# Where a layer's large tiles start in SBUF, and when its v, bias tables and combination take their turn

## The chip, the cores and the metric

One core of one Trainium2 chip. The metric is the time of one execution on the device in microseconds; smaller is better. The kernel before has a median of 1522.92 us over 3 runs (1522.58 to 1523.85).

## The reference

One layer of an encoder on 1024 tokens of width 1024, all in fp32. Cut to what matters:

```python
mod = silu(c) @ w_ada + b_ada                        # six vectors: sh1, sc1, gt1, sh2, sc2, gt2
h = rms_norm(x, g_norm1) * (1 + sc1) + sh1
qa, ka, va, qb, kb, vb, gates = split(h @ w_in)
o_a = neighbourhood_attention(rms(qa), rms(ka), va, rpb)      # 8 heads, bias, column mask
outs, lses = three dilated windows of rotary(rms(qb)), rotary(rms(kb)), vb    # 4 heads each
o_b = sum over windows of softmax(lses) * outs               # the combination
ga, gb = split(sigmoid(gates + b_gate))
x = x + gt1 * ((ga * (o_a @ w_proj_a) + gb * (o_b @ w_proj_b)) @ w_o)
h2 = rms_norm(x, g_norm2) * (1 + sc2) + sh2
a, up = split(h2 @ w_ffn_in)
x = x + gt2 * ((silu(a) * up) @ w_ffn_out)
```

## The kernel before, in words

Every large product is made of fp32r matmuls (a faster fp32 form) in three passes: each operand is split into a rounded part and the rest, whi and wlo for weights (`wsplit`, L108 on ACT and L109 on DVE or POOL), hT[0] and hT[1] for activations, and PASS multiplies high by high, high by low and low by high. In `nc.tensor.matmul(out, a, b)` the tile a is loaded into TensorE (PE) and b streams through it, 384 or 512 columns of 4 bytes.

The stages, in order of time:

- A prologue (to about 60 us) reads x and the first conditioning weights, and makes hT.
- Units 0 to 9, steps n = 6 to 79 of one loop (`u, t = divmod(n, 8)`, L897): in each step `proj_chunk` (L293) makes q, k and v of one token tile for the current unit, eight chunks of three matmuls with 384 columns of whi or wlo streaming. Between the chunks stands the attention of the unit before: `at_scores` (L451, L518: qk streams), `at_qk` (softmax, L465 to L469), the transposes of P (L477), `at_pv` (L492). At the end of a step `proj_post` normalizes q and k and stores v to v_d (L333); at t == 7 it loads the whole unit's v back (L344, eight DMAs for most units). Units 0 to 5 are the dilated windows (kinds 0 to 2), 6 to 9 the neighbourhood attention (kind 3), whose scores get a bias table rb per head (L398, 128x768). From step 58 on (PAIRED) each step has scores; a unit's scores begin two steps after its projections end.
- Beside this, `ada_step` runs once a step: it loads two rows of the conditioning weights (tile wa2, L276, 512 KB; the profile calls it wa) and multiplies them into acc2 on DVE (L280, L282; acc in the profile).
- The combination of the three windows: `combine_prep` loads a piece of the outputs (L626 to L633) and spreads its weights (fb), `combine_step` transposes fb on PE (four transposes, L647, into bank t) and multiplies. Twelve pieces, one a step, from `n - 63`: prep in steps 63 to 74, step in 64 to 75.
- Gates: L687, L706 (hT or tg stream); merge: L1095 (oT streams); output projection: L1237 (whi, wlo or wr streams); feed-forward: L1301 (h2T or t streams, whi or wlo is loaded) and L1471 (whi and wlo stream).

PE, ACT, DVE, POOL and SP (the DMA queue) take their instructions in an order fixed when the program is built; for the loop above a list scheduler sets that of ACT, DVE, POOL and SP, with priorities by the order of the code and `urgent`. A DMA into a tile waits on SP until the tile is free, and holds what is queued behind it. Eight buffers of 4096 bytes a partition, tag "big", hold v, rb, wa2, the pieces tp, gsig and oacc in turn; a tile that is asked for later takes its buffer later.

Where the tiles lie in SBUF (byte offset in each partition, modulo 512, in the built programs):

| tiles | before | addresses before | after |
|---|---|---|---|
| hT, h2T, raw, whi, wlo, x, x2 | 320 | 2,368 to 121,152 | 0 |
| qk, v, wa2, rb, PT, acc2, tp | 352 | 123,232 to 227,680 | 0 |
| P, stg | 416 | 191,392 to 205,728 | 0 |
| tg, sg, oT, wr, t, e, c, m | 480 | 139,232 and up | 0 |
| xt, tm, gt1, qn, rtab | 0 | 146,944 and up | 0 |
| ident | 448 | 1,472 | 448 |

Of the kernel before, what the change touches and what calls it, by code (L numbers as in the profile page):

```python
# [10 lines left out]
F32 = mybir.dt.float32  # L11
# [20 lines left out]
LATE, NPRE = (3, 4, 5, 6, 7), 12  # L32
KFIRST, KLAST, OT = (3, 4, 2, 0, 5, 6, 1, 7), (2, 0, 1, 3, 4, 5, 6, 7), 3
PP, QT, AQ, AT, AV = 100, 0, 0, 0, 0
WARM = 40
PAIRED = 58
XSQ = "avavaaaa"
XSC = "ddddvvvv"
XE = ("av", "vv", "aa", "aa", "vv", "aa", "va", "va")
# [3 lines left out]
def hybrid_layer(ctx: ExitStack, tc: tile.TileContext, x, colp, wada1, wada2, bada2, wqkv, wg, wpa, wpb,  # L43
                 wo, w1, w2, hgain, ropeg, rope, rbias, bmask, g2r, out):
    nc = tc.nc

    def pool(name, side, **kw):
        return tc.alloc_tile_pool(name=name, bufs=1, side=side, reuse_waits="tile", **kw)

    const = pool("const", "left")  # L50
    wp = pool("w", "left")
    ctx.enter_context(tc.manual_schedule(engines={mybir.EngineType.PE}))
    ps = tc.alloc_tile_pool(name="ps", bufs=2, space=bass.MemoryType.PSUM)
# [10 lines left out]
    x2_d = tc.dram_tile([S, D], F32, name="x2_d")  # L64
    w1_d = tc.dram_tile([2, 4, 128, 512], F32, name="w1_d")
    e_d = tc.dram_tile([6, 2, 128, 512], F32, name="e_d")

    def bank(tag):
        return ps.tile([128, 512], F32, tag=tag, name="ps_" + tag)
# [22 lines left out]
    nc.vector.tensor_mul(cact, cact, c_c)  # L92
    bg1 = const.tile([128, 8], F32, name="bg1")
    nc.vector.scalar_tensor_tensor(bg1, bsc1, 1.0, g1_c, op0=ALU.add, op1=ALU.mult)

    def fview(ap):
        return ap.bitcast(F32)
# [17 lines left out]
    def rstd(p, n, width, ss, tag):  # L115
        v = p.tile([128, width], F32, tag="rv", bufs=3, name="rv")
        y = p.tile([128, width], F32, tag="ry", bufs=3, name="ry")
        z = p.tile([128, width], F32, tag="rz", bufs=3, name="rz")
        nc.scalar.activation(y, ss, AF.Ln, scale=1.0 / n, bias=eps)  # L119
        nc.vector.tensor_scalar(v, ss, 1.0 / n, EPS, op0=ALU.mult, op1=ALU.add)  # L120
        nc.scalar.activation(y, y, AF.Exp, scale=-0.5)
        nc.vector.tensor_mul(z, y, v)
        nc.vector.scalar_tensor_tensor(z, z, -0.5, y, op0=ALU.mult, op1=ALU.mult)
        nc.vector.scalar_tensor_tensor(y, z, 1.5, y, op0=ALU.add, op1=ALU.mult)
        return y
# [7 lines left out]
    ap_ = pool("attn", "right")  # L133
# [7 lines left out]
    def big(name, shape=None, dtype=F32):  # L141
        return ap_.tile(shape or wide, dtype, tag="big", bufs=NBIG, name=name)

    yT = [ap_.tile([128, 4, S], F32, tag="qk", bufs=2, name="yT") for _ in range(2)]
    land = [big("land") for _ in range(NLAND)]
    seq = [0]

    def landing():
# [30 lines left out]
    pw = bank("t")  # L179
    for i in range(WARM):  # L180
        nc.tensor.transpose(pw[:, :128], ident, ident)
# [55 lines left out]
    rtab = []  # L237
# [8 lines left out]
                                        rg[:, qk, f, None, :].to_broadcast([128, 8, 16]), op=ALU.mult)  # L246
        return tb

    rg = const.tile([128, 2, 2, 16], F32, name="rg")
    nc.sync.dma_start(rg, ropeg)  # L250
    bm = ap_.tile([128, 512], F32, tag="bm", bufs=1, name="bmask")
    nc.sync.dma_start(bm, bmask)
# [43 lines left out]
    def urgent(off):  # L296
        def deco(f):
            def g(*a):
                with tc.high_priority(off):
                    return f(*a)  # L300
            return g
        return deco

    @urgent(PP)
    def proj_post(U, t):
        pd = U.pd[t]
        qn = ap_.tile([128, 4, 64], F32, tag="qn", bufs=7, name="qn")
        U.qn[t] = qn
        pq = pd[:, :256].rearrange("p (h d) -> p h d", h=4)
        sq = ap_.tile([128, 256], F32, tag="sq", bufs=1, name="sq")  # L310
        nc.scalar.activation(sq, pd[:, :256], AF.Square)
        nc.scalar.activation(qn, pq, AF.Copy)
        ss = ap_.tile([128, 4], F32, tag="ss4", bufs=2, name="ss4")
        nc.vector.tensor_reduce(ss, sq.rearrange("p (h d) -> p h d", h=4), axis=mybir.AxisListType.X, op=ALU.add)  # L314
        r = rstd(ap_, 64, 4, ss, "q")
        nc.vector.tensor_tensor(qn, qn, r[:, :, None].to_broadcast([128, 4, 64]), op=ALU.mult)  # L316
        if U.kind < 3:
            ra = ap_.tile([128, 4, 16], F32, tag="ra", bufs=2, name="ra")
            rb = ap_.tile([128, 4, 16], F32, tag="rb", bufs=2, name="rb")
            tb = U.tab[:, t]  # L320
            v4 = lambda z: z.rearrange("p (a b) c -> p a b c", a=2)
            tv = lambda f, c0, c1: tb[:, f, :, None, c0:c1].to_broadcast([128, 2, 2, c1 - c0])
            nc.gpsimd.tensor_tensor(v4(ra), v4(qn[:, :, 0:16]), tv(0, 0, 16), op=ALU.mult)  # L323
            nc.gpsimd.tensor_tensor(v4(rb[:, :, 0:8]), v4(qn[:, :, 8:16]), tv(1, 0, 8), op=ALU.mult)
            nc.gpsimd.tensor_tensor(v4(rb[:, :, 8:16]), v4(qn[:, :, 0:8]), tv(1, 8, 16), op=ALU.mult)
            nc.gpsimd.tensor_tensor(qn[:, :, 0:16], ra, rb, op=ALU.add)
        if U.kind == 0:
            nc.scalar.activation(U.v[:, t, :], pd[:, 256:384], AF.Copy)
        else:
            vs = ap_.tile([128, 128], F32, tag="vs", bufs=2, name="vs")  # L330
            nc.scalar.activation(vs, pd[:, 256:384], AF.Copy)  # L331
            vd = v_d[U.u - 2]
            nc.sync.dma_start(vd[t * 128:(t + 1) * 128, :], vs)  # L333
            if t == 7 and U.kind == 1:
                vv = vd.rearrange("(h i r) d -> h i r d", h=2, r=4)
                uv = U.v.rearrange("p (r h) d -> p h r d", h=2)
                for j in range(2):
                    nc.sync.dma_start(uv[:, j], vv[j])
            elif t == 7 and U.kind == 2:
                nc.sync.dma_start(U.v, vd.rearrange("(i u) d -> i u d", u=8))  # L340
            elif t == 7:
                vv = vd.rearrange("(r j c) d -> j c r d", r=16, c=8)
                for j in range(8):
                    nc.sync.dma_start(U.v[:, j, :], vv[j])  # L344
# [37 lines left out]
    def new_unit(u, w):  # L382
        U = Unit()
        U.kind, U.pair = UNITS[u]
        U.u = u
        U.w = w
        U.pd, U.qn = {}, {}
        qk = ap_.tile([128, 4, S], F32R, tag="qk", bufs=2, name="qk")
        U.qk = [qk[:, i, :] for i in range(4)]
        U.v = big("v", [128, 8, 128])  # L390
        if U.kind < 3:
            U.tab = rtab[0] if rtab else None
            U.st = ap_.tile([128, 9, 4], F32, tag="st", bufs=2, name="st")
        else:
            U.bias = []
            for h in range(2):
                b = big("rb", [128, 768])
                nc.sync.dma_start(b, rbias[U.pair * 2 + h])  # L398
                U.bias.append(b)
        return U  # L400

    class Item:
        pass
# [347 lines left out]
    extra = {}  # L751
    w0 = []
    U = new_unit(0, w0)
    units.append(U)
    rowk = {}
# [134 lines left out]
    for t in range(6):  # L890
        proj_post(U, t)
# [5 lines left out]
    for n in range(6, 92):  # L897
        u, t = divmod(n, 8)
        if u < 10:
            if t == 0:  # L900
                units.append(new_unit(u, [nextw[u, k] for k in range(KT)]))
            U = units[u]
            chunks = [lambda k=k, U=U, t=t: proj_chunk(U, t, k) for k in range(KT)]
        elif n - 80 < NPRE:
            chunks = gate_pre(n - 80)
        else:
            chunks = []
# [11 lines left out]
                    ready.setdefault(8 * u + 2 + slot, []).append(I)  # L919
        if n == 8 * 7 + 5:  # L920
            combine_stats()
        ci = n - (8 * 7 + 7)
        if 0 <= ci < 12:
            combine_prep(ci)
        if n >= PAIRED:
            done, prev, cur = prev, cur, ready.pop(n, [])
# [9 lines left out]
        def chunk():  # L936
            if chunks:
                chunks.pop(0)()
                k = 8 - len(chunks)
                if t == 7 and u + 1 < 10 and k < 8 and k >= 2:  # L940
                    nextw[u + 1, k] = wsplit(raws[u + 1, k], nc.vector if k % 2 else None)

        turns = [(units[0], tt) for tt in {8: (0, 1), 9: (2, 3), 11: (4, 5), 13: (6, 7)}.get(n, ())]
        if PAIRED <= n <= 81 or 9 < n < PAIRED and n % 2:
            turns += [(units[m // 8], m % 8) for m in ((n - 2,) if n >= PAIRED else (n - 3, n - 2)) if m >= 8]
        chunk()
# [3 lines left out]
        if n < 10:  # L950
            while chunks:
                chunk()
        if n >= PAIRED or n % 2 or n < 10:
            for I in cur:
# [35 lines left out]
            chunk()  # L990
        if u < 10:
            proj_post(U, t)

    def gate_first(i, eng):
        for q, nm in enumerate(("w11", "w12")):
            gwt[i, nm] = wsplit(gate_raw(i, q), eng)
# [188 lines left out]
    wop = pool("wo", "right")  # L1185
# [45 lines left out]
    for t in range(8):  # L1231
# [8 lines left out]
                o_turn(t - 2)  # L1240
        o_post(t, pbs)

    wj = {}

    gt = {}
# [285 lines left out]
    fp.release()  # L1531
    ps.release()
    wp.release()
    const.release()


# [98 lines left out]
```

## Time and profile before

| what | us |
|---|---|
| median of the runs | 1522.92 |
| the profiled execution's own time | 1524.07 |
| its span | 1522.3 |
| PE busy | 1499.0 |
| DVE busy | 1101.9 |
| ACT busy | 657.4 |
| POOL busy | 538.4 |

The mean granted clock of PE was 0.998. Matmuls are pipelined: the duration of one contains part of the one before, so their price is read from start to start. Bracketed times in the timeline are the wait ahead of an instruction, with what ended it. By stretches the span divides into the prologue (0 to 60), units with dilated attention (60 to 350), units with neighbourhood attention and the combination (350 to 520), gates (520 to 710), merge and output projection (710 to 875), and the feed-forward product (875 to 1522).

### The profile page before, as it was taken

Reading aid. Unit: us, or ns where it says so; the run is one execution under the profiler, and the core shown is the slowest. Engines: PE = TensorE matmul, PEld = TensorE weight load, DVE = VectorE, ACT = ScalarE, POOL = GpSimd, SP = SyncE. Lnnn points to the kernel's source line nnn. Section 1 sums busy time; section 2 is a strip of 40 time slices with the busy share of each in tenths; the row PEclk is TensorE's granted clock in tenths of the full one; section 3 lists DMA queues with packets and bytes.
Section 4 is the critical chain, followed back from the end, with each engine's and each line's share of the span. In section 5 each row is a group of like instructions: output and inputs, shape, how many; then the busy total and the mean of one; then the engine's idle time right before and its main releaser. Section 6 shows DMA issues by size and latency. Waiting matters only on the chain. (4 is left out here: it accounts for less than half of the span.)

```text
span 1522.3 us, 24290 instructions
## 1 busy us (share of the span) xinstructions
PE 1499.0 (98%) x8156; PEld 1267.7 (83%) x8156; DVE 1101.9 (72%) x2318; ACT 657.4 (43%) x1638; POOL 538.4 (35%) x540
## 2 busy tenths in 40 slices
PE   9999999999999999999999999999999999999998
PEld 7999989998888877788888888888888888887886
DVE  6868777767899845466665596788777777599468
ACT  5555555554544543236432354333222233344442
POOL 0432333311101040002342301677777775104464
PEclk9999999999999999999999999999999999999999
DMA  9625544535245165824562225345533334798342
GB/s 369 231 76 184 158 148 150 175 124 166 73 138 149 61 202 155 304 83 126 165 217 101 93 89 177 127 132 170 174 107 104 105 107 141 268 365 285 99 153 97
DMA packets 154414, 241.66 MB, mean 159 GB/s; under 512 B 26656, under 2 KB 73376, under 8 KB 153520
## 3 DMA queue, kind: packets, MB, share of 16 engines
q1 hardware_dynamic: 153136, 235.90, 47.5%
q10 hardware_dynamic: 1152, 4.19, 0.7%
q8 instruction: 65, 1.06, 0.3%
q14 instruction: 61, 0.50, 0.1%
HBM read 179.89 MB, written 60.15 MB: 158 GB/s over the span
## 5 line engine op out<-in xcount | busy, mean ns | idle before, releaser
L109 POOL TENSOR_TENSOR wlo<-raw,whi 128x512 fp32r<-128x512 f32 (+2 forms) x133 | 173.0, 1314 | 469.4 <-ACT whi L108 417.6
L108 ACT ACTIVATE whi<-raw 128x512 fp32r<-128x512 f32 (+1 forms) x348 | 204.3, 600 | 282.7 <-PE ps_s L1471 33.6
L293 PE MATMUL ps_d<-whi,hT 128*128 128x384 f32 x1152 | 311.7, 342 | 0.3 <-ACT vs L331 0.3
L109 DVE TENSOR_TENSOR wlo<-raw,whi 128x512 fp32r<-128x512 f32 (+1 forms) x215 | 181.8, 857 | 77.2 <-ACT whi L108 72.0
L293 PEld LDWEIGHTS ps_d<-whi,hT 128*128 128x128 f32 x1152 | 210.4, 189 | 5.8 <-ACT vs L331 4.1
L293 PE MATMUL ps_d<-wlo,hT 128*128 128x384 f32 x576 | 193.9, 337 | 2.2 <-DVE wlo L109 1.9
L293 PEld LDWEIGHTS ps_d<-wlo,hT 128*128 128x128 f32 x576 | 109.0, 189 | 3.0 <-DVE wlo L109 2.2
L108 ACT ACTIVATE whi<-ws 128x512 fp32r<-128x512 f32 x65 | 40.9, 629 | 130.3 <-DVE ws L1318 76.6
L1251 POOL TENSOR_TENSOR e<-e,c 128x512 f32<-128x512 f32 x44 | 68.6, 1560 | 64.3 <-DVE c L1381 40.1
L109 POOL TENSOR_TENSOR wlo<-m,whi 128x512 fp32r<-128x512 f32 x35 | 51.6, 1484 | 54.0 <-ACT whi L108 54.0
L323 POOL TENSOR_TENSOR ra<-qn,rtab 128x64 f32<-128x64 f32 x48 | 16.2, 338 | 150.8 <-DVE qn L316 132.1
L530 ACT ACTIVATE P<-P,st 128x256 f32<-128x256 f32 (+2 forms) x100 | 45.5, 456 | 40.6 <-DVE st L528 40.6
L687 PE MATMUL ps_d<-hT,whi 128*128 128x512 f32 x192 | 60.5, 396 | 0.0
L1301 PE MATMUL ps_v<-h2T,whi 128*128 128x512 f32 x192 | 59.3, 390 | 0.0
L1301 PE MATMUL ps_s<-h2T,whi 128*128 128x512 f32 x192 | 59.2, 390 | 0.0
L466 ACT ACTIVATE P<-P,sx 128x384 f32<-128x384 f32 (+1 forms) x64 | 37.0, 578 | 51.4 <-DVE sx L465 51.4
L1249 ACT ACTIVATE e<-e 128x512 f32<-128x512 f32 x44 | 27.4, 630 | 71.9 <-DVE e L1384 47.4
L282 DVE SCALAR_TENSOR_TENSOR acc<-wa,cact,acc 128x512 f32<-128x512 f32 x56 | 42.0, 749 | 20.6 <-DMA wa<-in_wada_dram 20.4
L1301 PE MATMUL ps_d<-h2T,whi 128*128 128x512 f32 x184 | 56.8, 390 | 0.0
L109 DVE TENSOR_TENSOR wlo<-ws,whi 128x512 fp32r<-128x512 f32 x45 | 50.5, 1123 | 8.2 <-ACT whi L108 8.2
L119 ACT ACTIVATE ry<-ss,eps 128x4 f32<-128x4 f32 (+1 forms) x88 | 26.3, 299 | 67.4 <-DVE ss L314 65.2
L1250 DVE TENSOR_TENSOR e<-e 128x512 f32<-128x512 f32 x44 | 42.6, 975 | 17.3 <-ACT e L1249 17.1
(445 smaller groups left out, 3968.9 us busy)
## 6 DMA issues: line engine op xcount, KB each, us to landing
raw<-in_w_dram SPq DMA_DIRECT2D x139, 256.0 KB
ga_d<-e SPq DMA_DIRECT2D x77, 256.0 KB
raw<-ga_d SPq DMA_DIRECT2D x77, 256.0 KB
wa<-in_wada_dram SPq DMA_DIRECT2D x32, 512.0 KB
raw<-in_wqkv_dram SPq DMA_DIRECT2D x80, 192.0 KB
m<-in_w_dram SPq DMA_DIRECT2D x44, 256.0 KB
raw<-in_wg_dram SPq DMA_DIRECT2D x42, 256.0 KB
xt<-in_x_dram SPq DMA_DIRECT2D x16, 512.0 KB
```

Source lines behind the costliest of these rows:

```text
L108: nc.scalar.activation(hi[:, :n], r, AF.Copy)
L109: (eng or nc.gpsimd).tensor_sub(lo[:, :n], r, fview(hi[:, :n]))
L119: nc.scalar.activation(y, ss, AF.Ln, scale=1.0 / n, bias=eps)
L282: nc.vector.scalar_tensor_tensor(ada_acc[c], wa, cact[:, kk:kk + 1], ada_acc[c], op0=ALU.mult, op1=ALU.add)
L293: nc.tensor.matmul(pd[:, :384], tok(a, k, t), U.w[k][b][:, :384], start=(k == 0 and i == 0), stop=(k == KT - 1 and i == 2))
L466: nc.scalar.activation(P[:nq, :nk], P[:nq, :nk], AF.Exp, scale=-1.0, bias=nm, accum_out=sm)
L530: nc.scalar.activation(C.P[h][:nq, c], C.P[h][:nq, c], AF.Exp, scale=-1.0, bias=nm, accum_out=sm)
L687: nc.tensor.matmul(st["p"], gw[i, br][j][a][:, kk * 128:(kk + 1) * 128], hT[b][:, k, hs], start=(k == 0 and q == 0), stop=(k == 7 and q == 2))
L1249: nc.scalar.activation(sg, a, AF.Sigmoid)
L1250: nc.vector.tensor_mul(sg, sg, a)
L1251: nc.gpsimd.tensor_mul(sg, sg, up)
L1301: nc.tensor.matmul(pb, w[p][:, k * 128:(k + 1) * 128], b[q][:, k], start=(k == 0 and i == 0), stop=(k == 3 and i == 2))
```

## The change

Four edits, cut to their core:

```diff
+EDGE, CFILL, AFILL, OFILL = 480, 192, 384, 32
-PAIRED = 58
+PAIRED, RBT, COMB = 58, 5, 64
...
+    edge = pool("edge", "right")
+    edge.tile([128, EDGE // 4], F32, name="edge")
...
+    def fill(p, n, name):
+        p.tile([128, n // 4], F32, name=name)
...
+    rg = const.tile([128, 2, 2, 16], F32, name="rg")
+    fill(const, CFILL, "cfill")
...
+    for tag, n, bufs in (("bm", 512, 1), ("p", 512, 4), ("qn", 256, 7), ("rtab", 512, 1), ("acc2", 512, 1), ("pT", 512, 4),
+                         ("stg", 512, 3), ("vs", 128, 2), ("ra", 64, 2), ("rb", 64, 2)):
+        ap_.tile([128, n], F32, tag=tag, bufs=bufs, name="place")
...
+            if t == 7:
+                U.v = big("v", [128, 8, 128])
             if t == 7 and U.kind == 1:
...
-        U.v = big("v", [128, 8, 128])
+        if U.kind == 0:
+            U.v = big("v", [128, 8, 128])
...
             U.bias = []
-            for h in range(2):
-                b = big("rb", [128, 768])
-                nc.sync.dma_start(b, rbias[U.pair * 2 + h])
-                U.bias.append(b)
...
+    def bias_tabs(U):
+        for h in range(2):
+            b = big("rb", [128, 768])
+            nc.sync.dma_start(b, rbias[U.pair * 2 + h])
+            U.bias.append(b)
...
-        ci = n - (8 * 7 + 7)
+        ci = n - COMB
...
             proj_post(U, t)
+            if U.kind == 3 and t == RBT:
+                bias_tabs(U)
+
+    fill(ap_, AFILL, "afill")
...
+    fill(wop, OFILL, "ofill")
```

1. Unused tiles (edge, cfill, afill, ofill) and the list of tags taken early, large before small, put every large tile at a multiple of 512 bytes. Nothing writes or reads them.
2. v takes its big buffer just ahead of its load at t == 7 instead of at the unit's start (kind 0, which writes it from PSUM, excepted).
3. The two bias tables of a kind-3 unit are allocated and loaded at the end of its step 5 instead of at its start.
4. The combination's pieces stand one step later: prep in steps 64 to 75, step in 65 to 76.

The order on POOL is the same as before. On PE only the transposes of the combination move. Lines of the new program are 10 to 18 higher (L276 becomes L288, L282 L294, L293 L305, L465 L482, L398 L416, L344 L358, L647 L664).

On SP, around the turn from unit 6 to unit 7 (v and v_d are the unit's values, rb the bias tables, wa2 the conditioning weights, u_d a window's output), before:

```order
L344 DMA v_4679<-v_d_72 128x1x128 x8
L333 DMA v_d_72<-vs_5360 128x128
L398 DMA rb_5310<-in_rbias_dram 128x768
L398 DMA rb_5312<-in_rbias_dram 128x768
L276 DMA wa2_5341<-in_wada2_dram 128x1024
L573 DMA u_d_70<-stg_5387 128x512
L333 DMA v_d_72<-vs_5429 128x128
L276 DMA wa2_5486<-in_wada2_dram 128x1024
L276 DMA wa2_5666<-in_wada2_dram 128x1024
```

and after:

```order
L358 DMA v_5314<-v_d_76 128x1x128 x8
L345 DMA v_d_76<-vs_5370 128x128
L288 DMA wa2_5351<-in_wada2_dram 128x1024
L590 DMA u_d_74<-stg_5397 128x512
L288 DMA wa2_5496<-in_wada2_dram 128x1024
L288 DMA wa2_5676<-in_wada2_dram 128x1024
L345 DMA v_d_76<-vs_5439 128x128
L416 DMA rb_5815<-in_rbias_dram 128x768
L416 DMA rb_5817<-in_rbias_dram 128x768
L288 DMA wa2_5910<-in_wada2_dram 128x1024
```

Here the three wa2 loads moved ahead of the two rb loads, the first of them to the place of the first rb.

On DVE in step 59, where the first of these wa2 tiles is used (acc2 is the running sum; rz, ry and qn belong to the normalization of q and k; the ISA rows read the scores of two heads with their bias; P is the softmax), before:

```order
L123 SCALAR_TENSOR_TENSOR rz_5421<-rz_5421,ry_5420 128x4
L124 SCALAR_TENSOR_TENSOR ry_5420<-rz_5421,ry_5420 128x4
L316 TENSOR_TENSOR qn_5413<-qn_5413,ry_5420 128x256
L465 ISA P_5455,sx_5456<-ps_s_5447,rb_4680 128x256
L465 ISA sx_5456 128x1
L465 ISA P_5461,sx_5462<-ps_s_5448,rb_4682 128x256
L465 ISA sx_5462 128x1
L379 SCALAR_TENSOR_TENSOR qk_5308<-ps_v_5467,hg_83,qk_5308 128x2x64
L380 TENSOR_TENSOR qk_5308<-ps_v_5467,qk_5308 128x2x64
L468 RECIPROCAL sx_5456<-sx_5456 128x1
L282 SCALAR_TENSOR_TENSOR acc2_5119<-wa2_5341,cact_96,acc2_5119 128x512
L469 TENSOR_SCALAR P_5455<-P_5455,sx_5456 128x256
```

and after:

```order
L133 SCALAR_TENSOR_TENSOR rz_5431<-rz_5431,ry_5430 128x4
L294 SCALAR_TENSOR_TENSOR acc2_5129<-wa2_5351,cact_100,acc2_5129 128x512
L134 SCALAR_TENSOR_TENSOR ry_5430<-rz_5431,ry_5430 128x4
L482 ISA P_5465,sx_5466<-ps_s_5457,rb_5150 128x256
L482 ISA sx_5466 128x1
L482 ISA P_5471,sx_5472<-ps_s_5458,rb_5152 128x256
L482 ISA sx_5472 128x1
L294 SCALAR_TENSOR_TENSOR acc2_5129<-wa2_5351,cact_100,acc2_5129 128x512
L328 TENSOR_TENSOR qn_5423<-qn_5423,ry_5430 128x256
L393 SCALAR_TENSOR_TENSOR qk_5323<-ps_v_5477,hg_87,qk_5323 128x2x64
L394 TENSOR_TENSOR qk_5323<-ps_v_5477,qk_5323 128x2x64
L485 RECIPROCAL sx_5466<-sx_5466 128x1
```

The first use of the tile moved from behind both score passes to ahead of ry.

On PE in step 64 (whi and wlo stream against hT; fb holds the combination's weights), before:

```order
L293 MATMUL ps_d<-whi,hT_106 128x384
L293 MATMUL ps_d<-wlo,hT_106 128x384
L293 MATMUL ps_d<-whi,hT_391 128x384
L647 MATMUL ps_t<-ident,fb 128x128 x4
L293 MATMUL ps_d<-whi,hT_106 128x384
```

and after, the same place:

```order
L305 MATMUL ps_d<-whi,hT_112 128x384
L305 MATMUL ps_d<-wlo,hT_112 128x384
L305 MATMUL ps_d<-whi,hT_406 128x384
L305 MATMUL ps_d<-whi,hT_112 128x384
L305 MATMUL ps_d<-wlo,hT_112 128x384
```

The four transposes are gone from this step; the row x4 stands in each of the steps 65 to 76 now.

More of the change, by code (lines that the diff above doesn't have):

```diff
@@ L247, in rope_tab @@
         return tb
-    rg = const.tile([128, 2, 2, 16], F32, name="rg")
     nc.sync.dma_start(rg, ropeg)
@@ L1533, in hybrid_layer @@
     wp.release()
+    edge.release()
     const.release()
```

## The prediction

> **What bounds the kernel now.** I read the page's busy times first, then the stretches, then the matmul groups with shapes kept apart, then the timeline of single matmuls, and last the list of waits. The page says that TensorE (PE) is nearly the whole span, at an almost full clock:
>
> ```profile
> span 1522.3 us, 24290 instructions
> PE 1499.0 (98%) x8156; PEld 1267.7 (83%) x8156; DVE 1101.9 (72%) x2318; ACT 657.4 (43%) x1638; POOL 538.4 (35%) x540
> PEclk9999999999999999999999999999999999999999
> ```
>
> By stretches (the columns are busy time and instructions of PE, its weight loads, DVE, ACT and POOL, then granted clock, DMA share, GB/s):
>
> ```profile
> 350.00:520.00 170.00, 162.40 (x1140) 143.35 (x1139) 147.34 (x490) 87.59 (x293) 14.41 (x13) 0.99 0.41 124
> 700.00:760.00 60.00, 60.00 (x260) 48.48 (x259) 42.84 (x59) 31.93 (x48) 24.84 (x20) 1.00 0.49 156
> 760.00:860.00 100.00, 100.00 (x454) 81.63 (x453) 57.40 (x100) 29.58 (x68) 32.96 (x20) 1.00 0.39 139
> 950.00:1360.00 410.00, 410.00 (x1783) 334.94 (x1782) 309.25 (x363) 131.81 (x223) 252.44 (x175) 1.00 0.48 158
> ```
>
> The reader is to see two kinds of time. From 700 on PE is busy without a gap while DVE has 101 of 410 us to spare, POOL 158 and DMA half: there only the length of a matmul counts, and a shorter one shortens the kernel at once. From 350 to 520 (units 6 to 9, with the combination) PE waits 7.6 us and DVE is busy 87%: there the order of other engines counts. The change touches both, so I cost them apart. A difference of 0.2%, 3.0 us, is about what a measurement of this kernel can tell from no change.
>
> **Edit 1: large tiles at multiples of 512 bytes.** It adds no instruction but unused memory. What it can alter is how long an instruction reads or writes a tile. In the matmul groups the operand behind "<-" that comes first is the one that streams through (512 columns of the tile), the second is the loaded one; the last number is the mean ns.
>
> ```profile
> L293 PE MATMUL ps_d<-whi,hT 128*128 128x384 f32 x1152 | 311.7, 342 | 0.3 <-ACT vs L331 0.3
> L1301 PE MATMUL ps_v<-h2T,whi 128*128 128x512 f32 x192 | 59.3, 390 | 0.0
> L1301 PE MATMUL ps_d<-t,whi 128*128 128x512 f32 x136 | 42.8, 396 | 0.0
> ...
> L1301 PE MATMUL ps_s<-t,whi 128*128 128x512 f32 x128 | 40.3, 396 | 0.0
> ...
> L1301 PE MATMUL ps_v<-t,wlo 128*128 128x512 f32 x68 | 27.0, 397 | 0.0
> ...
> L1301 PE MATMUL ps_t<-t,wlo 128*128 128x512 f32 x64 | 25.4, 396 | 0.0
> ...
> L1237 PE MATMUL ps_d<-wr,h2T 128*128 128x512 f32 x90 | 22.4, 398 | 0.0
> ...
> L1095 PE MATMUL ps_v<-oT,whi 128*128 128x512 f32 x64 | 20.2, 397 | 0.0
> ...
> L706 PE MATMUL ps_v<-hT,whi 128*128 128x512 f32 x48 | 14.8, 389 | 0.0
> ...
> L706 PE MATMUL ps_d<-tg,whi 128*128 128x512 f32 x40 | 12.6, 396 | 0.0
> ```
>
> One line, L706, issues the same matmul from hT in 389 ns and from tg in 396; L1301 does so from h2T and t. By their places in memory (front part), hT, h2T, whi and wlo start at 320 past a multiple of 512, tg, t, oT and wr at 480. 320 is a multiple of 64, 480 is not. These durations overlap, since matmuls are pipelined, so the price is read from starts:
>
> ```profile
> 949.33 0.62 PE L1301 MATMUL ps_d<-h2T,whi 128*128 128x512 f32 x2
> ...
> 951.37 0.63 PE L1301 MATMUL ps_s<-t,whi 128*128 128x512 f32 x2
> ...
> 956.91 0.63 PE L1301 MATMUL ps_v<-t,whi 128*128 128x512 f32 x2
> ...
> 959.72 0.63 PE L1301 MATMUL ps_d<-t,whi 128*128 128x512 f32 x2
> ```
>
> From 949.33 to 951.37 stand nine matmuls from h2T: 2.04 / 9 = 226.7 ns from start to start. From 956.91 to 959.72 stand twelve from t: 2.81 / 12 = 234.2 ns. The tile at 480 costs some 7 ns more each. How many there are: from t 136 + 136 + 128 + 128 on whi and half as many on wlo (each pass runs twice on whi, once on wlo), 792; from wr 90 + 90 + 60 = 240; from oT 288 and from tg 180, of which the rows above are the largest groups. Together 1,500, and 1,500 x 7 ns = 10.5 us. The difference in a start is known to about 1 ns, so 9 to 12. All lie in stretches where PE has no gap, or next to it, so I count all of it; DVE's and POOL's slack above covers a step that is 3% shorter.
>
> The score matmuls read qk, now at 352, also not a multiple of 64:
>
> ```profile
> L451 PE MATMUL ps_s<-qk 64*128 64x384 f32 x144 | 19.0, 368 | 0.0
> ```
>
> With L518's and the smaller groups they are 492 matmuls of 64 rows, which run in pairs, 246 pairs. The start of what they read varies inside the tile, and no row has the same form at another place. From nothing to the full 7 ns a pair is 0 to 1.7 us; I take the middle, 0.9.
>
> The rest, the tiles at 320 that go to 0, I cost at nothing, because 320 is already a multiple of 64 and the matmuls from it are the shorter. That is a choice; the first rival is its failure. DVE, ACT and POOL read and write the same tiles; their groups of 128x512 at 320 and at 480 differ by no step that I could see, and PE would hide it from 700 on.
>
> **Edits 2 to 4: the order in units 6 to 9.** v's big buffer is taken later, but its load stays where it was on SP's queue. What moves is what else waits on those buffers. The bias tables rb (two of 393 KB) go from the start of a unit to its sixth step, behind the wa loads instead of ahead. Step 59 shows what that order costs now (the bracket is the wait ahead of the instruction):
>
> ```profile
> 364.87 0.90 SPq L398 DMA_DIRECT2D rb<-in_rbias_dram  x2
> 365.87 0.37 SPq L276 DMA_DIRECT2D wa<-in_wada_dram  x1
> ```
> ```profile
> 371.93 0.75 DVE L282 SCALAR_TENSOR_TENSOR acc<-wa,cact,acc 128x512 f32<-128x512 f32 x1 [4.39 <-DMA wa<-in_wada_dram]
> ```
> ```profile
> 373.01 0.44 PE L477 MATMUL ps_t<-ident,P 128*128 128x128 f32 x2 [1.77 <-DVE P L469]
> 374.32 0.44 PE L477 MATMUL ps_t<-ident,P 128*128 128x128 f32 x2 [0.88 <-DVE P L469]
> ```
>
> SP, done with v's eight pieces, issues rb and then wa. wa arrives 6 us after its issue, acc waits 4.39 us for it on DVE, and P, behind acc, holds PE's transposes for 1.77 + 0.88 = 2.65 us. Now wa is issued where rb was, 1.0 us earlier (365.87 - 364.87), with 786 KB less ahead of it. That speaks for a gain of up to these 2.65 us, plus what the clock lost after it, which I estimate at 1 to 2 us. But the new order on DVE puts acc earlier too (front part): ry, qn and both score passes, which it stood behind, now stand behind acc. If wa lands 2 us earlier and acc stands 2 us earlier, the wait is as long as before and only falls on other work. Gain 3, loss 3 at the ends; I take 1.0, since the issue is earlier for sure. The rb loads come five steps before the first scores that read them (a unit's scores begin two steps after its end): hidden.
>
> The combination begins at step 65 instead of 64. Step 64 also carries the last weight splits of the next unit and the load of v:
>
> ```profile
> 414.90 0.66 PE L647 MATMUL ps_t<-ident,fb 128*128 128x128 f32 x4 [1.67 <-ACT PT L483]
> ```
>
> The first four transposes of L647 wait 1.67 us for a bank that ACT frees. Moved on, they meet a step with less in it: 1.5 us gained, if nothing else is late in step 64. In exchange the last combination lies in step 76, which now has one piece more; 0 to 1 us lost if that step waits too, which DVE's 87% allows. Its output is read only by L1095's oT after 700. Together the order edits are worth 2.5 us, between a gain of 6.5 (both waits and their clock) and a loss of 4.
>
> **Sum.** The profiled execution took 1524.07 us (span 1522.3), 1.15 above the median of the runs, 1522.92. 1524.07 - 10.5 - 0.9 - 2.5 = 1510.2; against the median, 1509.0. By the ends of the terms: 1522.92 - 12 - 1.7 - 6.5 = 1502.7 and 1522.92 - 9 + 4 = 1517.9.
>
> **Rivals.** *First, the granule is coarser than 64 bytes, and the tiles at 320 pay as well.* Then the 226.7 ns would also fall. A second step of 7 ns for the L293 matmuls (1,152 from whi, 576 from wlo), the 1,056 from h2T, those of L1471 (924) and the other tiles at 320 (some 800), 4,500 in all, is 31.5 us, and 7 more on the 1,500 is 10.5: 1509 - 42 = 1467. No large tile that streams through PE starts at 0 now, so the trace has no row against it; for it speaks only that 226.7 ns has no reason of its own here. I hold it less likely, because the one step that the rows show is used up between 320 and 480. The Trainium skill, TensorE: Matmul & The Clock Gate, section "Wait — 56ns, not 53.3ns?", gives 215.7 ns from start to start for 512 columns when warm (measured there on bf16); this trace has 226.7 at its best place, so by that page 11 ns would still be open on every matmul, about 66 us over 6,000, as an estimate. Nothing here shows whether the type or the place makes that gap. From 1475 down the producers would begin to bind (DVE is at 309 of 410 us), so I give this case 1445 to 1480. Chance 0.17.
>
> *Second, the address modulo 64 isn't the reason.* The tiles with the longer matmuls all lie in the upper half of the memory (t from 139,232 up), the others below 122,000; the trace cannot tell which property does it. If it is the half, edit 1 is worth nothing, and with -2.5 to +1 of the order the time is 1520.4 to 1524; I say 1521.5. By the Trainium skill, SBUF — State Buffer, section "Specifications (TRN2)", SBUF is read in lines of 16 bytes: 320 and 480 are both multiples of 16, so by that rule the two would cost the same and edit 1 would bring nothing; the rows above, 389 against 396 ns on one line, show that something beyond that rule separates them. Chance 0.13.
>
> *Third, slower: acc becomes a wait ahead of everything.* wa competes with v's eight pieces and lands as late as now. DVE reaches acc before ry, qn, scores and P, and the whole 4.39 us goes to PE with some 1.5 us of lost clock, 5.9 us, in each of the three units 7, 8 and 9: 17.7. Against the 11.4 of edit 1 that is +6.3: 1529. It decides when wa lands more than 4 us after DVE gets to acc in all three. The wait row above speaks for it; that wa is issued ahead of rb speaks against. Chance 0.08.
>
> **How the numbers follow.** The forecast has 0.62, own range 1503 to 1518; the rivals 0.17, 0.13 and 0.08. Faster by over 0.2%: 0.62 + 0.17 and a little of the second, 0.80. Within: nearly all of the second, 0.12. Slower: the third, 0.08. The range leaves out the first rival (0.17) and the far end of the third, and takes in the others: 1502 to 1527.
>
> **What would show it.** Right: the groups of t, tg, oT and wr at 389 to 390 ns, the twelve matmuls of 956.91 at 2.72 us; L293 unchanged at its pitch; the stretch from 700 to 1360 shorter by about 9 us, that from 350 to 520 by 2 to 3, with no wait of L647 in step 64. Wrong: L1301 from h2T or L1471 shorter than now (first rival), t still at 396 (second), acc waiting longer on wa and PE's wait in 350 to 520 above 7.6 us (third).

## The result, and the profile after

Five runs of the changed kernel took 1509.84 us in the median (1508.57 to 1516.15), against 1522.92 (1522.58 to 1524.86) for five of the kernel before: a ratio of 0.9921, with an interval of 0.9900 to 0.9942. The profiled execution took 1508.57 us. The page of the changed kernel:

```profile
span 1506.8 us, 24296 instructions
PE 1486.2 (99%) x8156; PEld 1265.3 (84%) x8156; DVE 1098.1 (73%) x2318; ACT 656.3 (44%) x1638; POOL 537.1 (36%) x540
```

The span is 15.5 us shorter; PE is busy 12.8 us less with the same 8,156 matmuls. The matmul groups with shapes kept apart (the last number is the mean ns):

```profile
L1323 PE MATMUL ps_v<-h2T,whi 128*128 128x512 f32 x192 | 59.2, 389 | 0.0
...
L1323 PE MATMUL ps_v<-t,whi 128*128 128x512 f32 x136 | 41.9, 389 | 0.0
...
L1258 PE MATMUL ps_d<-wr,h2T 128*128 128x512 f32 x90 | 21.7, 391 | 0.0
...
L1116 PE MATMUL ps_v<-oT,whi 128*128 128x512 f32 x64 | 19.7, 389 | 0.0
...
L468 PE MATMUL ps_s<-qk 64*128 64x384 f32 x144 | 19.3, 369 | 0.0
...
L723 PE MATMUL ps_d<-tg,whi 128*128 128x512 f32 x40 | 12.3, 389 | 0.0
```

All four groups that stood at 396 to 398 are at 389 to 391; h2T is where it was, and the score matmuls too (368 before, 369 now). From start to start, in the timeline:

```profile
944.20 0.61 PE L1323 MATMUL ps_s<-t,whi 128*128 128x512 f32 x2
...
946.92 0.61 PE L1323 MATMUL ps_t<-h2T,whi 128*128 128x512 f32 x2
```

Twelve matmuls of t take 2.72 us, 226.7 ns each, where they took 2.81. Where in the span the time went is read from when each stage's first matmul starts (a tile's instructions: min, median and max duration, then first and last start). Before:

```profile
L706 PE MATMUL ps_s<-tg,whi x32: 392/397/400, 632.8 to 702.9; 128*128 128x512 f32 x32
L1471 PE MATMUL ps_d<-whi x88: 388/389/397, 1302.9 to 1511.7; 128*128 128x512 f32 x88
```

After:

```profile
L723 PE MATMUL ps_s<-tg,whi x32: 389/389/389, 632.4 to 699.9; 128*128 128x512 f32 x32
L1493 PE MATMUL ps_d<-whi x88: 388/389/431, 1289.6 to 1497.4; 128*128 128x512 f32 x88
```

Up to tg, behind all the units and the combination, this execution is ahead by 0.4 us; at the start of the last product it is ahead by 13.3, so 12.9 come between the two, where the matmuls got shorter; 2.2 more come behind that start. The 0.4 holds for this execution alone, the fastest of the five. In the repeat of the same kernel (below) tg starts 2.8 us later than before, and with the place edit alone 3.0 earlier:

```profile
L723 PE MATMUL ps_s<-tg,whi x32: 389/389/389, 635.6 to 703.5; 128*128 128x512 f32 x32
```
```profile
L721 PE MATMUL ps_s<-tg,whi x32: 389/389/389, 629.8 to 698.7; 128*128 128x512 f32 x32
```

So one profile does not price the order edits; the experiments do. Inside the units the stall of step 64 has gone, and a new one stands in step 66. On SP, DVE and PE of the changed kernel:

```profile
412.69 4.90 SPq L358 DMA_DIRECT2D v<-v_d  x8
...
418.62 0.42 SPq L288 DMA_DIRECT2D wa<-in_wada_dram  x1
```
```profile
423.69 1.54 DVE L294 SCALAR_TENSOR_TENSOR acc<-wa,cact,acc 128x512 f32<-128x512 f32 x2 [3.98 <-DMA wa<-in_wada_dram]
425.14 0.68 DVE L672 TENSOR_TENSOR oacc<-ut,ps_t 128x512 f32<-128x512 f32 x1
```
```profile
425.88 0.44 PE L494 MATMUL ps_t<-ident,P 128*128 128x128 f32 x2 [2.33 <-DVE oacc L672]
...
429.48 0.66 PE L664 MATMUL ps_t<-ident,fb 128*128 128x128 f32 x4 [1.05 <-ACT PT L500]
```

A piece of the combination (L672) stands behind acc on DVE, acc waits 3.98 us for a wa that was issued behind v's eight pieces, and the bank that L672 should free holds PE for 2.33 us. Step 64 became 2.3 us shorter, step 66 3.8 longer (first L293 or L305 to the next step's first). Step 59, the other stall, is still there, 10.40 us long for 9.72, with acc waiting 4.07 us. PE's wait from 350 to 520 is 8.1 us, where it was 7.6.

### The profile page after: what moved, and what is told of

The parts are those of the page before. It is cut to its first block, busy times and chain, and to the rows that moved or that the text cites. A ratio compares the mean times of both kernels' runs of the same rounds, so it can differ in the third digit from the quotient of the medians.

```text
span 1506.8 us, 24296 instructions
## 1 busy us (share of the span) xinstructions
PE 1486.2 (99%) x8156; PEld 1265.3 (84%) x8156; DVE 1098.1 (73%) x2318; ACT 656.3 (44%) x1638; POOL 537.1 (36%) x540
## 5 line engine op out<-in xcount | busy, mean ns | idle before, releaser
L305 PE MATMUL ps_d<-whi,hT 128*128 128x384 f32 x1152 | 311.0, 341 | 0.0
L305 PEld LDWEIGHTS ps_d<-whi,hT 128*128 128x128 f32 x1152 | 210.3, 189 | 5.3 <-ACT vs L343 3.5
L305 PE MATMUL ps_d<-wlo,hT 128*128 128x384 f32 x576 | 193.6, 336 | 2.4 <-DVE wlo L119 2.0
L305 PEld LDWEIGHTS ps_d<-wlo,hT 128*128 128x128 f32 x576 | 108.9, 189 | 3.2 <-DVE wlo L119 2.3
L294 DVE SCALAR_TENSOR_TENSOR acc<-wa,cact,acc 128x512 f32<-128x512 f32 x56 | 43.2, 772 | 24.6 <-DMA wa<-in_wada_dram 24.6
L1272 DVE TENSOR_TENSOR e<-e 128x512 f32<-128x512 f32 x44 | 42.5, 974 | 17.3 <-ACT e L1271 17.2
```

Of the source, the lines that this page charges most:

```text
L294: nc.vector.scalar_tensor_tensor(ada_acc[c], wa, cact[:, kk:kk + 1], ada_acc[c], op0=ALU.mult, op1=ALU.add)
L305: nc.tensor.matmul(pd[:, :384], tok(a, k, t), U.w[k][b][:, :384], start=(k == 0 and i == 0), stop=(k == KT - 1 and i == 2))
L1272: nc.vector.tensor_mul(sg, sg, a)
```

## The experiments

All ratios are to the kernel before on the same chip. The first four kernels separate the edits and test the reason given for the first.

**The place edit alone** (v, rb and the combination put back; the order of every engine is that of before):

```diff
-            if U.kind == 3 and t == RBT:
-                bias_tabs(U)
...
-        ci = n - COMB
+        ci = n - 63
```

> The tiles lie as after the change, the order of every engine is that of before. Theory one (the gain is the matmuls that stream a tile whose start is not a multiple of 64 bytes): 1,500 matmuls x 7.5 ns = 11.3 us less than before, so 1510 to 1512, with the groups of t, tg, oT and wr at 389 ns and the stall of step 64 still there. Rival (the order edits carry a good part): 1517 or more.

Measured: 1511.71 us against 1522.57, ratio 0.9921 (0.9906 to 0.9935). The whole gain of the change, 12.0 us by that ratio. t is at 389 ns. Its profile has the stall of step 64 as before, and between merge and output projection a wait that the profile of the changed kernel doesn't have (four other kernels here have it at 0.4 to 1.7 us):

```profile
PE ps_t L662 <- ACT PT L498: 1.7, 1, 1.7
```
```profile
PE ps_d L1254 <- DVE sg L1116: 3.7, 1, 3.7
```

This execution (span 1513.1) is the slowest of the kernel's six, which reach from 1508.91 to 1514.98, so it is not read for its sum.

**The order edits alone** (the fills and the early tags left out; order of every engine as after):

```diff
-    edge = pool("edge", "right")
-    edge.tile([128, EDGE // 4], F32, name="edge")
...
-    fill(const, CFILL, "cfill")
```

> The order of every engine is that of after the change, the tiles lie as before. Theory one: the order edits nearly cancel among themselves, 1520.5 to 1523, with t at 396 ns, no stall of the combination in step 64 and a new one in step 66. Rival (the order edits carry a good part): 1515 or less.

Measured: 1526.29 against 1522.57, ratio 1.0019 (1.0009 to 1.0029). They cost 2.9 us by themselves (1.4 to 4.4); neither theory had that. The stall of step 64 is gone, and step 66 is 10.93 us long, as expected. t is at 396 ns. DVE's waits on wa from 300 to 530 are 12.0 us before, 17.2 here.

**The lower half moved 32 bytes** (all else as after):

```diff
-EDGE, CFILL, AFILL, OFILL = 480, 192, 384, 32
+EDGE, CFILL, AFILL, OFILL = 480, 160, 384, 32
```

> After the change, with the tiles of the lower half (hT, h2T, raw, whi, wlo) moved 32 bytes down, to 480 past a multiple of 512; the upper half stays at 0. Theory one (any large streamed tile off a multiple of 64 pays, wherever it lies): some 4,500 matmuls x 7.5 ns = 34 us more than after, 1540 to 1546, with h2T at 396 ns and its twelve matmuls at 2.81 us. Rival (only the upper half pays for its offset): within 3 us of after, 1508 to 1513.

Measured: 1524.94 against 1522.57, ratio 1.0015 (1.0004 to 1.0027). Neither 34 us nor nothing. The groups tell why:

```profile
L1323 PE MATMUL ps_v<-h2T,whi 128*128 128x512 f32 x192 | 59.5, 391 | 0.0
L1323 PE MATMUL ps_v<-t,whi 128*128 128x512 f32 x136 | 42.7, 395 | 0.0
```

h2T, which now starts at 480 (32 past a multiple of 64), keeps nearly its 390 ns; t, which starts at 0, pays. My reason (an absolute multiple of 64) has fallen: t was not moved. What both kernels have in common is the difference between the tile that streams and the tile that is loaded: whi lies at 480 here, t at 0; before, whi at 320, t at 480. h2T and whi lie alike in both.

**The upper half moved to 32** (EDGE 448 for 480):

> After the change, with every large tile of the upper half moved to 32 past a multiple of 512; the lower half stays at 0. Theory one: the 1,500 matmuls pay again, 11.3 us more than after, 1519 to 1523, t at 396 ns. Rival (480 is bad for what is near its end, a line of 512 bytes, and 32 is not): within 3 us of after, t at 389 to 391 ns.

Measured: 1527.09, ratio 1.0031 (1.0018 to 1.0044). t pays again:

```profile
L1323 PE MATMUL ps_v<-t,whi 128*128 128x512 f32 x136 | 42.8, 395 | 0.0
```

By both theories this one had to be as it is, so it adds only that 32 is as bad as 480. The time is 17 us above after, more than the 11.3 expected. The matmul groups hold some 11 to 12 of them. In the profiles 3.3 of the rest lie in the units, but the repeat of the changed kernel is 3.2 behind its first profile there too, so the tiles' places need not be the reason. The new theory two, that the difference counts, went into the next four.

**Both halves at 480** (EDGE 0, no edge tile; CFILL 160):

> After the change, with all large tiles, of both halves, at 480 past a multiple of 512. Theory one (absolute: a streamed tile off a multiple of 64 pays): every group pays, some 6,000 matmuls x 7.5 ns = 45 us, 1550 or more. Theory two (relative: only a difference modulo 64 between the streamed and the loaded tile pays): as after, 1508 to 1514, t and h2T at 389 ns.

Measured: 1516.75 against 1523.64, ratio 0.9959 (0.9941 to 0.9976), far from 1550. The groups:

```profile
L1321 PE MATMUL ps_v<-h2T,whi 128*128 128x512 f32 x192 | 59.2, 389 | 0.0
L1321 PE MATMUL ps_v<-t,whi 128*128 128x512 f32 x136 | 41.9, 389 | 0.0
```

No matmul pays, with every tile off a multiple of 64. The absolute rule is dead; the relative one stands so far. The time is above the expected 1514; the changed kernel beside the last runs (0.9936, 0.9924 to 0.9949) overlaps with it, and the matmuls are equal, so no difference between the two is shown.

**The upper half at 64** (EDGE 416):

> After the change, with every large tile of the upper half moved to 64 past a multiple of 512; the lower half (hT, h2T, whi, wlo) stays at 0. Theory one (a start must be a multiple of 64) and theory two (the streamed tile and the loaded tile must agree modulo 64): as after, 1508 to 1514, t at 389 ns. Rival (they must agree to 128 or more): t at 396 ns and 1522 to 1528.

Measured: 1521.96 against 1523.64, ratio 0.9987 (0.9973 to 1.0001). Theory two with 64 bytes has failed as well:

```profile
L1323 PE MATMUL ps_v<-h2T,whi 128*128 128x512 f32 x192 | 59.6, 391 | 0.0
L1323 PE MATMUL ps_v<-t,whi 128*128 128x512 f32 x136 | 42.3, 392 | 0.0
```

A difference of 64 costs t about 3 ns (392 for 389) instead of 7, so the rival's 396 isn't reached either, and it costs h2T 2. By the means from start to start (t 229.8, h2T 229.0, against 226.7) that is 2.5 + 2.4 us, with wr, oT and tg some 6, half of the loss; the rest is in the units. h2T pays although it streams from 0 and all that it loads lies at 0. Three blocks of twelve matmuls from h2T, one after the other, behind a block from t:

```profile
1108.64 0.63 PE L1323 MATMUL ps_s<-h2T,whi 128*128 128x512 f32 x2
...
1111.41 0.62 PE L1323 MATMUL ps_t<-h2T,whi 128*128 128x512 f32 x2
...
1114.13 0.62 PE L1323 MATMUL ps_v<-h2T,whi 128*128 128x512 f32 x2
...
1116.85 0.63 PE L1323 MATMUL ps_d<-t,whi 128*128 128x512 f32 x2
```

The first takes 2.77 us (230.8 ns each), the second and the third 2.72 (226.7). So a price that began with t runs on into some of the matmuls behind it, although these agree; over the 45 runs of h2T matmuls in this stage, the first ten take some 232 ns on average and those after them 226.7.

**Three differences in one kernel** (the blocks t, renamed):

```diff
-        tb.append([tps[-1].tile([128, 4, 512], F32R, name=f"t{n}{i}") for i in range(2)])
+        o = (16, 48, 128)[n - 1] // 4
+        tb.append([tps[-1].tile([128, 2176], F32R, tag=f"t{n}{i}", name="u" + "abc"[n - 1])[:, o:o + 2048].rearrange("p (k n) -> p k n", k=4)
+                   for i in range(2)])
```

> After the change, with the three blocks t of the feed-forward stage (named ua, ub, uc here) started 16, 48 and 128 bytes past a multiple of 512; all else at 0. Modulo 64: ua and ub pay (230 to 235 ns from start to start), uc does not (227). Rival (only a difference of 32 bytes pays): all three 227. Rival (agreement to 512 is needed): all three pay.

Measured (one execution, 1520.7 us): all three pay. The starts of twelve matmuls each:

```profile
955.43 0.62 PE L1323 MATMUL ps_v<-ua,whi 128*128 128x512 f32 x2
...
958.21 0.63 PE L1323 MATMUL ps_d<-ub,whi 128*128 128x512 f32 x2
...
961.01 0.63 PE L1323 MATMUL ps_s<-h2T,whi 128*128 128x512 f32 x2
...
963.74 0.62 PE L1323 MATMUL ps_t<-uc,whi 128*128 128x512 f32 x2
...
966.53 0.63 PE L1323 MATMUL ps_v<-h2T,whi 128*128 128x512 f32 x2
```

16 bytes (ua): 2.78 / 12 = 231.7 ns. 48 (ub): 2.80 / 12 = 233.3. h2T between them: 2.73 / 12 = 227.5. 128 (uc): 2.79 / 12 = 232.5. So the streamed and the loaded tile must agree to more than 128 bytes; 256 was not tried, and a multiple of 512 is what before's h2T and all of after have in common.

**Only whi and raw moved, by 32 bytes** (in the weights' pool, a fill of 32 between whi and wlo, CFILL 160):

```diff
+    for tag, n in (("raw", NRAW), ("hi", NHL)):
+        wp.tile([128, 512], F32, tag=tag, bufs=n, name="place")
+    fill(wp, 32, "lofill")
+    wp.tile([128, 512], F32, tag="lo", bufs=NHL, name="place")
```

> After the change, with raw and whi at 480 past a multiple of 512, wlo and all else at 0, so that within each triple of matmuls (whi with the high part, whi with the low part, wlo with the high part) only the first two differ from the tile that streams. Theory two with the matmul's own loaded tile: the first two of a triple take 234 ns, the third 227. Theory two with the tile that is loaded for the next matmul while this one streams: the first and third 234, the second 227. Theory one (absolute): no matmul of t or h2T pays, 227 throughout.

Measured (one execution, 1534.07 us): every matmul pays, those on wlo too, though wlo agrees with what streams.

```profile
L1328 PE MATMUL ps_v<-h2T,whi 128*128 128x512 f32 x192 | 60.8, 397 | 0.0
L1328 PE MATMUL ps_v<-t,whi 128*128 128x512 f32 x136 | 43.0, 397 | 0.0
L1328 PE MATMUL ps_v<-h2T,wlo 128*128 128x512 f32 x96 | 37.7, 393 | 0.0
```

h2T pays as t does: nothing is special about the upper half. On wlo the price is 4 ns, on whi 8. Both forms of theory two wanted one member of the triple at 227; by the starts of all products the triple takes 236, 233 and 231 ns. The third differs only from the whi that is loaded while it streams, the second only from its own whi, the first from both. So both may count; or, as the kernel with the upper half at 64 suggests, the price of one member runs on into the next. These runs do not decide it.

The last four kernels, on one chip, are about the order.

**The changed kernel again:**

> The changed kernel once more, beside the next three. Theory (the order edits bring nothing on top of the place edit, and their waits on wa vary from run to run): 0.992 to 0.996 of before, 1510 to 1517, no better than the kernel with the place edit alone. Rival (the order edits bring the 2.5 us that were forecast): 0.992 or less, and at least 2 us below the kernel with the place edit and the later combination alone.

Measured: 1513.71 against 1523.68, ratio 0.9936 (0.9924 to 0.9949), as the theory has it: no better than the place edit alone (0.9921, another chip) or the next kernel. In this profile all three units stall, in steps 59, 66 and 74, which take 11.94, 9.56 and 11.27 us (8.49, 6.83 and 6.83 with the place edit alone). The wait of acc on DVE in step 59, and that of PE in step 74:

```profile
369.48 0.75 DVE L294 SCALAR_TENSOR_TENSOR acc<-wa,cact,acc 128x512 f32<-128x512 f32 x1 [5.21 <-DMA wa<-in_wada_dram]
```
```profile
489.46 0.66 PE L494 MATMUL ps_t<-ident,P 128*128 128x128 f32 x2 [3.02 <-DVE oacc L675]
```

**The place edit and the later combination, v and rb as before** (bias_tabs called in new_unit, v taken there):

> Place edit and the combination one step later; v and rb as in before. If the later combination by itself removes the stall of step 64 (1.67 us of wait, 2.3 us of the step): 0.990 to 0.9915 of before, 1507 to 1510. If the stall only moves to another step: 0.992, 1511, as the place edit alone.

Measured: 1513.76, ratio 0.9931 (0.9919 to 0.9943), no better than the changed kernel or the place edit alone. Step 64 is 6.74 us long instead of 8.99, but step 66 is 9.51 (6.83 with the place edit alone) and step 75 9.89 (8.33). In step 66 acc waits for wa again:

```profile
425.68 0.75 DVE L294 SCALAR_TENSOR_TENSOR acc<-wa,cact,acc 128x512 f32<-128x512 f32 x1 [3.92 <-DMA wa<-in_wada_dram]
```

So the later combination makes the stall of step 66 without the late v and rb. The rival of the expectation holds: the stall moves.

**The changed kernel with wa asked for one conditioning step earlier:**

```diff
         if kk % 2 == 0:
-            ada_acc["w"] = big("wa2", [128, 2, 512])
-            nc.sync.dma_start(ada_acc["w"], wada2[c, :, kk:kk + 2, :])
+            ada_acc["w"] = ada_acc["next"]
+        elif i < 63:
+            ada_load(i + 1)
```

> The changed kernel with each wa load asked for one conditioning step earlier (at the second use of the pair before). If the wait of acc on wa is what the order edits lose by: the waits of acc in 300 to 520 fall from 15.3 us to under 8, and the time to 1503 to 1507. If the buffers free up no earlier, so that the loads stay behind v: no change, 1508 to 1516.

Measured: 1511.02 against 1523.68, ratio 0.9927 (0.9901 to 0.9954); beside the changed kernel (0.9936) no difference is shown, and 1503 to 1507 was not reached. DVE's waits on wa from 300 to 530 are 12.1 us for 17.3, not the 8 that the first case asked for.

**The place edit alone with the same early wa:**

> The place edit alone (order of before) with each wa load asked for one conditioning step earlier. If waits on wa cost this order anything (10.7 us of DVE's time in 300 to 520): 2 to 5 us below the place edit alone, 1505 to 1509. If the buffers hold the loads back: no change, 1510 to 1513.

Measured: 1508.35, ratio 0.9900 (0.9886 to 0.9914), below the changed kernel beside it (0.9924 to 0.9949) without overlap: the best version measured, 5.4 us under it. Against the place edit alone (0.9906 to 0.9935, another chip) the intervals overlap. From 350 to 520 (the place edit with early wa, the changed kernel of the same chip, the place edit alone):

```profile
350.00:520.00 170.00, 164.77 (x1177) 144.98 (x1176) 148.96 (x502) 88.80 (x298) 14.55 (x14) 1.00 0.39 121
```
```profile
350.00:520.00 170.00, 161.10 (x1119) 141.66 (x1118) 144.12 (x482) 85.90 (x288) 14.68 (x13) 0.97 0.40 123
```
```profile
350.00:520.00 170.00, 163.63 (x1173) 144.33 (x1170) 148.83 (x503) 88.52 (x296) 14.97 (x14) 1.00 0.40 124
```

In the same 170 us PE gets through 1,177 matmuls instead of 1,119, and keeps its full clock. Of these 58 more, 54 stand in the profile of the old order alone (1,173); the early wa adds 4. And DVE still waits 12.8 us for wa, more than with the place edit alone (10.7): what it gains is not the wait's length, as I had expected, but where acc stands. SP issues wa no earlier than before (367.2); in step 59 acc now stands behind both rows of P (L492) instead of ahead of them, and though it waits 4.24 us (4.07 with the place edit alone), the step is 5.70 us long (8.49 with the place edit alone, 11.94 in the changed kernel). Whether that shortens the whole kernel is not shown.

## Why the prediction was right, and where it was wrong

The number was 1509.0; measured were 1509.84 and, in the repeat, 1513.71. Sign and range were right, and so was the place: stretches in which PE has no gap. From the first matmul of oT to the start of the last product the profile is 10.3 us shorter (about 9 forecast); the 2 to 3 us of the units did not come. By its steps:

- *Edit 1, 10.5 us.* Right in size, wrong in reason, and so right by luck in who pays. The 1,500 matmuls of t, wr, oT and tg went from 234.2 to 226.7 ns, 7.5 each: 11.3 us; the place edit alone measured 12.0. But the step "320 is a multiple of 64, 480 is not" failed: with all tiles at 480 nothing pays, with the upper half at 64 t pays. The price belongs to the difference between the tile that streams and the tile that is loaded, to more than 128 bytes, and runs on into some matmuls behind. I had seen only pairs in which the two explanations give the same groups. The 226.7 ns of before came from nine matmuls of h2T; the three ahead of them, next to t, took 230 each (0.69 us from 948.64).
- *The tiles at 320, nothing.* Right, for the new reason: hT, h2T, whi and wlo lay alike. The first rival was half true: the granule is coarser than 64 bytes, yet those tiles had nothing to gain, and 226.7 ns stayed. The 215.7 that the Trainium skill (TensorE: Matmul & The Clock Gate, "Wait — 56ns, not 53.3ns?") gives was not reached here by any place.
- *The second rival, the upper half,* is out: t in the upper half runs at 389 ns after the change, and h2T in the lower pays 397 once whi differs. The 16-byte lines of the Trainium skill (SBUF — State Buffer, "Specifications (TRN2)") do not bear on it: 16, 48 and 64 bytes, all multiples of 16, cost 3 to 7 ns.
- *The scores, 0.9 us.* Nothing: 369 ns after, 368 before. What streams and what is loaded there are both pieces of one qk tile, which moved as a whole; that this is the reason was not tested.
- *The order edits, 2.5 us gained.* Wrong in sign: alone they cost 2.9 us (1.4 to 4.4), and on top of the place edit no gain is shown (0.9921 and 0.9936 with, 0.9921 without). "If nothing else is late" was the weak place: step 64 gave 2.3 us, and the piece moved on met an acc that waits 3 to 4 us for wa in step 66. At step 59 of the first profile wa was issued 0.57 us behind v's last piece instead of 1.56, the 1.0 us that was foreseen, but DVE reached acc earlier as well, so its wait shrank only from 4.39 to 4.07 and fell on scores and qn; in the repeat it is 5.21. That is the third rival's mechanism, and both its signs came: acc waits on wa from 300 to 530 for 15.3 us (repeat 17.3), where it was 12.0, and PE's wait from 350 to 520 is 8.1 (repeat 8.9) for 7.6. It struck in each of the three units, in steps 59, 66 and 73 to 74, but at some 3 us instead of 17.7.

The number was near because edit 1 carries 10.5 of its 13.9 us, and the price of that edit was read from rows that hold under either rule. The 3.4 us of the scores and the order did not come, edit 1 brought 0.8 to 1.5 more than forecast, and the some 2 us that are left lie inside the measured interval (8.8 to 15.2 us gained).

## What to carry to other kernels

Look at matmul groups that differ only in a tile, by start to start, and then at both tiles' addresses: a few ns on each of 1,500 matmuls were 12 us in stretches where TensorE never waits. One alignment for all large tiles is the safe choice, since it makes every pair agree; before believing a rule about one tile, move the other one. An operation that waits for a DMA should stand in its engine's queue behind what others wait for: with the same wait of some 4 us, step 59 took 5.70 us with acc behind P and 8.49 with acc ahead of it (one profile each). And one profile is not enough to price an order: the same kernel reached tg at 632.4 us in one and at 635.6 in another.

## What the runs showed of the hardware

A 512-column fp32r matmul took 226.7 ns from start to start when the tile that streams and the tile that is loaded agree modulo 512 bytes (both at 0, at 320 against 320, at 480 against 480). With a difference of 16 bytes it took 231.7, of 32 some 233.5, of 48 233.3, of 64 some 230, of 128 232.5, of 160 234.2. A matmul that agrees pays too near others that differ: 231 ns on wlo with whi moved by 32, and 230.8 in the first block of twelve from h2T behind t at a difference of 64, with 226.7 in the next. A difference of 256 was not tried in these products.
